# Attention in a four-part decoder trunk: one value product a pair of heads over 512 queries at causal widths, instead of two over 256

## The chip, the cores and the metric

The kernel runs on one core of one Trainium2 chip. The metric is the device time of one execution in microseconds, as a median of several runs. Below, PE is TensorE, DVE is VectorE, ACT is ScalarE, POOL is GpSimd and SP is SyncE, the engine that issues the loads of weights. All times and traces are of this chip.

## What is computed

The input is a sequence of 512 tokens with 1024 features, in float32. Two layers follow each other: an attention mixer with a gated feed-forward part, and a short-convolution mixer with the same feed-forward part. Only the attention mixer is changed:

```python
xn = rms_norm(h, norm_g)
proj = xn @ w_in                       # q, k, v of 16 heads of 64, and 8 gate logits
q_fox, k_fox, q_sb, k_sb = ...         # each head's q and k normalised over 64
# heads 0-7, forgetting attention:
logits = q @ k.T * scale + cum_f[q] - cum_f[k]        # causal: key <= query
out = softmax(logits) @ v
# heads 8-15, stick-breaking attention:
z = q @ k.T * scale                                   # strict: key < query
w = exp(log_sigmoid(z) + sum of log_sigmoid(-z) over later keys)
out = w @ v
h = h + concat(out) @ w_out
```

## The kernel before, in words

**Precision.** Every product of two float32 matrices is made of three matmuls. Each operand is split into a high part (`hi`, rounded to the type that PE reads fast, written by ACT) and the rest (`lo`, a subtraction on DVE); the matmuls are hi x hi, lo x hi and hi x lo (`mm3`, L246 to L252, and `mm3_rhs`, L502 to L505). Weights arrive by a DMA of 512 KB into `raw` and are split into `whi` and `wlo` (L227, L228).

**Layout.** Activations lie with features in partitions and the 512 tokens in columns. The 16 heads are worked on in 8 pairs, p = 0 to 7; pairs 0 to 3 are forgetting attention (`fox`), pairs 4 to 7 stick-breaking. Queries go in blocks of 128, b = 0 to 3.

**The steps of a pair.**
- `queries_keys(p)` makes K and Q of a pair: 24 matmuls of 512 columns for each (L248 to L250), an eviction with squares (L585, L593), then some microseconds of other work later the sums of squares (`sums`, L539), their turn (L547), the inverse roots on small tiles (`scales`, L549 to L568), and, ROWS microseconds later by the kernel's own counter, the turn of the widened scales (`rows`, L575) and the scaled Q and K (L577, L339, L340).
- `values(g)` makes V of four heads (two pairs): 4 blocks of 24 matmuls of 256 columns (L503 to L505).
- `logits(p, b)` makes the logits of one query block for both heads of a pair. Each head uses 64 of the array's 128 rows, so the two heads' matmuls run side by side (L610, L614). It goes on with the softmax (L625 to L630) or the stick-breaking weights (two sigmoids, a scan and a product, L634 to L640). Each head has its own tile `w`, and in stick-breaking its own `rest`.
- `turn(p, b)` turns a block's weights, 128 x 128 at a time, into a PSUM bank (L659) and splits them into the tiles `pt` (L662, L663). A `pt` tile holds two query blocks (256 queries) for 4 key blocks. The key blocks that the first of the two queries' blocks may not see are filled with zeros by POOL (L653).
- `weigh(p, half)` is the value product of 256 queries: for each head 2 (first half) or 4 (second half) key blocks, twice each for `hi` and `lo`, 256 columns wide (L678, L679). Both heads share one PSUM bank. The stationary operand is V's hi and lo side by side, so the two halves of the result are added (L688, L689) and split into `o_hi` and `o_lo`.
- `output` is the output projection of heads 0 to 7 with its residual add (L727), `output_part` that of heads 8 to 15.

**PSUM.** There are eight banks in three rings (`bank`, L69): "a" with two banks, "b" with four, "c" with two. K, Q, V, the value product and the output projection take "a"; logits take "b"; turns, sums and scales take "c".

**The order.** It is made by the kernel's own counter of PE time (`spend`, `after`, `fill`, L177 to L198). A loop over the 32 blocks issues the logits of block g, then FILL1 microseconds of other work (`fillers`: K, Q and V of later pairs, later the output projection), the value product of a block pair that is ready, the turns of block g - 1, then FILL2 microseconds of fillers. A scheduler below the kernel may move an instruction by some places. Weights are loaded in the order of a list (`want`).

Of the kernel before, what the change touches and what calls it, by code (L numbers as in the profile page):

```python
# [50 lines left out]
def trunk(  # L51
# [207 lines left out]
    class Norm:  # L259
# [222 lines left out]
    def values(g):  # L482
# [3 lines left out]
        for b in range(NB):  # L486
            acc = bank("a")
# [19 lines left out]
    rx2 = const.tile([P, NB], F32, tag="rx2", name="rx2")  # L507

    def square_norm():
        dve.tensor_tensor(rx2, norm.col, norm.col, op=ALU.mult)  # L510
        dve.tensor_scalar(rx2, rx2, 1.0 / HD, None, op0=ALU.mult)
# [8 lines left out]
    def queries_keys(p):  # L520
# [3 lines left out]
        v = tiny.tile([P, NB, 2, 2], F32, tag="qv", name=f"qv{p}")  # L524
        r = tiny.tile([P, NB, 2, 2], F32, tag="qr", name=f"qr{p}")
# [7 lines left out]
        def sums():  # L533
# [7 lines left out]
            flat = work.tile([P, 2 * P], F32, tag="flat", name=f"flat{p}", bufs=1)  # L541
# [13 lines left out]
        def scales():  # L555
            vf, rf = (t.rearrange("p b i h -> p (b i h)") for t in (v, r))
            dve.tensor_scalar(vf, vf, EPS, None, op0=ALU.add)
            rsqrt(rf, vf, 16, f"qk{p}")
            rf = r.rearrange("p b i h -> p b (i h)")
            dve.tensor_tensor(rf, rf, norm.col[:, :, None].to_broadcast([P, NB, 4]), op=ALU.mult)  # L560
            if not fox:
                s = q_scale[p] = aw.tile([P, 2, NB, 2], F32, tag="qscale", name=f"qscale{p}", bufs=3)
                dve.tensor_copy(s[:, 0], r[:, :, 1, :])
                dve.tensor_scalar(s[:, 1], r[:, :, 1, :], -1.0, None, op0=ALU.mult)
            wides = {}
            for i in kept:
                wides[i] = work.tile([P, S], F32, tag="u0", name=f"qwide{p}{i}").rearrange("p (b h d) -> p b h d", b=NB, h=2)
                dve.tensor_copy(wides[i], r[:, :, i, :][:, :, :, None].to_broadcast([P, NB, 2, HD]))  # L568
# [12 lines left out]
        for i in range(2):  # L581
            acc = bank("a")
# [12 lines left out]
        after(SUMS, sums)  # L595

    def logits(p, b):
# [20 lines left out]
        ws = []  # L618
        for e in range(2):
            s = ss[e]  # L620
            w = aw.tile([P, S], F32, tag="w", name=f"w{p}{b}{e}", bufs=WB)
            ws.append(w)
            if fox:
                top = tiny.tile([P, 1], F32, tag="top", name=f"top{p}{b}{e}")
                dve.reduce_max(top, s[:, 0:n], axis=AX.X, negate=True)  # L625
# [4 lines left out]
                dve.tensor_scalar(w[:, 0:n], w[:, 0:n], inv, None, op0=ALU.mult)  # L630
            else:
                scale = q_scale[p]
                rest = aw.tile([P, S], F32, tag="rest", name=f"rest{p}{b}{e}")
                act.activation(rest[:, 0:n], s[:, 0:n], AF.Sigmoid, scale=scale[:, 1, b, e:e + 1])  # L634
                act.activation(w[:, 0:n - 1], s[:, 0:n - 1], AF.Sigmoid, scale=scale[:, 0, b, e:e + 1])

                pool.memset(w[:, n - 1:n], 0.0)
                back = rest[:, 1:n][:, ::-1]
                dve.tensor_tensor_scan(back, back, begin[:, S - n + 1:S][:, ::-1], 0.0, op0=ALU.mult, op1=ALU.max)  # L639
                dve.tensor_tensor(w[:, 0:n - 1], w[:, 0:n - 1], rest[:, 1:n], op=ALU.mult)  # L640
        return ws
# [3 lines left out]
    def turn(p, b, ws):  # L645

        half, n = b // 2, (b + 1) * P
        if b % 2 == 0:
            pts[p, half] = []
            for e in range(2):  # L650
# [3 lines left out]
                pts[p, half].append(both)  # L654
        at_ = slice((b % 2) * P, (b % 2 + 1) * P)
        for e in range(2):
            t = bank("c")
            for k in range(b + 1):
                pe.transpose(t[:, k * P:(k + 1) * P], ws[e][:, k * P:(k + 1) * P], ident)  # L659
            src = t[:, 0:n].rearrange("p (k q) -> p k q", q=P)  # L660
            hi, lo = pts[p, half][e]
            act.activation(hi[:, 0:b + 1, at_], src, AF.Copy)  # L662
            dve.tensor_tensor(lo[:, 0:b + 1, at_], src, f32(hi[:, 0:b + 1, at_]), op=ALU.subtract)  # L663
        spend(0.22 * (b + 1))

    def weigh(p, half):
# [4 lines left out]
        acc = bank("a")  # L671
        to = slice(half * 256, (half + 1) * 256)
        last = 2 * half + 1
        for e in range(2):
            hi, lo = pts[p, half][e]
            for k in range(last + 1):
                w = v[:, k, 2 * (p % 2) + e].rearrange("p i d -> p (i d)")
                pe.matmul(acc[:, e * 256:(e + 1) * 256], w, hi[:, k, :], start=k == 0, stop=False)  # L678
                pe.matmul(acc[:, e * 256:(e + 1) * 256], w, lo[:, k, :], start=False, stop=k == last)  # L679
        spend(0.44 * (last + 1))  # L680
        if p == 4 and half == 0:
            o_tiles[1] = mixed(1)
        o_hi, o_lo = o_tiles[p // 4]
        total = work.tile([P, S], F32, tag="y", name=f"o{p}{half}")[:, 0:256]
        for e in range(2):
            own, other = (slice(i * HD, (i + 1) * HD) for i in (e, 1 - e))
            cols = slice(e * 256, (e + 1) * 256)
            act.activation(total[own, :], acc[other, cols], AF.Copy)  # L688
            dve.tensor_tensor(total[own, :], acc[own, cols], total[own, :], op=ALU.add)  # L689
        split(o_hi[:, p % 4, to], o_lo[:, p % 4, to], total)  # L690
# [120 lines left out]
    after(NORM0, lambda: (norm.scale(sums0), square_norm()))  # L811
# [6 lines left out]
    aw = attn.enter_context(tc.tile_pool(name="aw", bufs=2))  # L818

# [5 lines left out]
    dr = ap_.tile([P, S], F32R, tag="dr", name="dr")  # L825
# [6 lines left out]
    for g, ps_ in enumerate(((1, 2), (3, 4), (5, 6), (7,))):  # L832
# [6 lines left out]
    for g in range(len(blocks) + 2):  # L839
# [6 lines left out]
        if g >= 2 and blocks[g - 2][1] % 2:  # L846
            p, b = blocks[g - 2]
# [165 lines left out]
```

## Time and profile before

| | |
|---|---|
| runs of before | 1220.8, 1221.25, 1221.3 us, median 1221.25 |
| the profiled execution | 1220.77 us |
| its span, first to last instruction | 1219.0 us |
| TensorE's granted clock | 1.00 |
| attention | about 25 to 280 us of the span |

The profile shows one execution. A group's row has the line, the engine, the operation, tiles (out<-in), the shape, the count, then the busy time and the mean of one, and behind a bar the idle time of the engine just ahead of them with what ended it. A row of the timeline begins with the start and the duration. PE's rows overlap: a matmul starts while the one ahead is still in the pipeline, so the distance between starts is what a matmul costs in a stream, and the row's own length is not.

### The profile page before, as it was taken

The numbers are of one execution on the slowest core, as the hardware profiler recorded it, in microseconds if no ns is written. First come the engines' busy times: TensorE is split into PE (matmuls) and PEld (weight loads), VectorE is DVE, ScalarE is ACT, GpSimd is POOL, SyncE is SP. The second block draws the span as 40 slices with busy tenths as digits, with TensorE's granted clock in tenths as the row PEclk, the third lists the DMA queues.
The fourth block names the chain that finished last, engine by engine and source line by source line (L and its number), as shares of the span: only waits on it lengthen the run. The fifth ranks groups of instructions, "written<-read, shape, count | busy, mean of one in ns | idle before, by whom it ended". The sixth has DMA issues, their size and how long they took to land.

```text
span 1219.0 us, 15006 instructions
## 1 busy us (share of the span) xinstructions
PE 1204.0 (99%) x5841; PEld 973.4 (80%) x5841; DVE 762.8 (63%) x1250; ACT 503.4 (41%) x787; POOL 26.6 (2%) x139
## 2 busy tenths in 40 slices
PE   8999999999999999999999999999999999999998
PEld 7887877778888888888888888888888888888886
DVE  5887888887867777663333555465776767672222
ACT  6556576655544443432222222233434344442120
POOL 4000000000000000000000000000000000000000
PEclk9999999999999999999999999999999999999999
DMA  7312121213233333323333333323233332322330
GB/s 196 88 36 70 36 69 36 70 62 96 87 102 89 97 93 94 96 81 93 94 95 104 89 102 87 104 87 104 87 93 98 89 102 87 103 87 88 121 102 35
DMA packets 182696, 108.14 MB, mean 89 GB/s; under 512 B 4732, under 2 KB 175020, under 8 KB 182624
## 3 DMA queue, kind: packets, MB, share of 16 engines
q1 hardware_dynamic: 182080, 106.94, 29.7%
q8 instruction: 46, 0.75, 0.3%
q0 software_dynamic: 384, 0.17, 0.1%
q14 instruction: 26, 0.21, 0.1%
q10 hardware_dynamic: 160, 0.07, 0.0%
HBM read 105.06 MB, written 2.10 MB: 88 GB/s over the span
## 4 chain that ended last, share of the span: by engine, by line
PE 91%; DVE 6%; ACT 2%; issue 1%; DMA 0%; SPq 0%; DVEq 0%; POOL 0%; ACTq 0%
PE psa L248 13%; PE psa L250 12%; PE psa L249 12%; PE psb L248 12%; PE psb L250 12%; PE psb L249 12%; PE psa L503 2%; PE psa L504 2%; PE psa L505 2%; PE psb L504 2%; PE psb L503 2%; PE psb L505 2%; DVE rest L639 1%; PE psc L659 1%; PE psb L610 1%
## 5 line engine op out<-in xcount | busy, mean ns | idle before, releaser
L227 ACT ACTIVATE whi<-raw 128x1024 fp32r<-128x1024 f32 (+3 forms) x199 | 208.9, 1050 | 362.7 <-PE psb L249 134.9
L228 DVE TENSOR_TENSOR wlo<-raw,whi 128x1024 fp32r<-128x1024 f32 (+3 forms) x199 | 240.4, 1209 | 160.2 <-ACT whi L227 159.1
L248 PE MATMUL psa<-hs_hi,whi 128*128 128x512 f32 x544 | 219.4, 403 | 2.5 <-DVE o L689 1.3
L250 PE MATMUL psa<-hs_hi,wlo 128*128 128x512 f32 x544 | 215.1, 395 | 0.2 <-DVE wlo L228 0.2
L249 PE MATMUL psa<-hs_lo,whi 128*128 128x512 f32 x544 | 214.6, 395 | 0.0
L248 PE MATMUL psb<-hs_hi,whi 128*128 128x512 f32 x480 | 189.9, 396 | 0.0
L250 PE MATMUL psb<-hs_hi,wlo 128*128 128x512 f32 x480 | 189.8, 395 | 0.0
L249 PE MATMUL psb<-hs_lo,whi 128*128 128x512 f32 x480 | 188.7, 393 | 0.0
L347 DVE SCALAR_TENSOR_TENSOR u<-y,taps,u 128x510 f32<-128x510 f32 (+1 forms) x176 | 131.1, 748 | 3.3 <-ACT u L344 0.4
L248 PEld LDWEIGHTS psa<-hs_hi,whi 128*128 128x128 f32 x544 | 102.3, 188 | 25.7 <-issue 2.3
L250 PEld LDWEIGHTS psa<-hs_hi,wlo 128*128 128x128 f32 x544 | 102.2, 188 | 25.0 <-DVE wlo L228 1.1
L249 PEld LDWEIGHTS psa<-hs_lo,whi 128*128 128x128 f32 x544 | 102.3, 188 | 22.2 <-DVE hs_lo L758 0.4
L249 PEld LDWEIGHTS psb<-hs_lo,whi 128*128 128x128 f32 x480 | 90.1, 188 | 21.4
L250 PEld LDWEIGHTS psb<-hs_hi,wlo 128*128 128x128 f32 x480 | 90.1, 188 | 21.4
L248 PEld LDWEIGHTS psb<-hs_hi,whi 128*128 128x128 f32 x480 | 90.3, 188 | 20.2
L885 DVE TENSOR_TENSOR y<-psb,nrow_n 128x512 f32<-128x512 f32 x44 | 30.4, 691 | 83.3 <-PE psb L250 83.3
L339 ACT ACTIVATE a<-u 128x512 fp32r<-128x512 f32 x44 | 27.9, 634 | 118.7 <-DVE u L890 118.7
L889 ACT ACTIVATE u<-u 128x512 f32<-128x512 f32 x44 | 27.9, 633 | 91.3 <-DVE u L347 91.3
L344 ACT ACTIVATE u<-y,taps 128x512 f32<-128x512 f32 x88 | 63.1, 719 | 1.2 <-DVE y L885 1.1
L340 DVE TENSOR_TENSOR a<-u,a 128x512 fp32r<-128x512 f32 x44 | 30.5, 692 | 29.4 <-ACT a L339 29.4
L503 PE MATMUL psa<-whi,hs_hi 128*128 128x256 f32 (+1 forms) x128 | 38.3, 299 | 0.8 <-ACT qk L593 0.7
L505 PE MATMUL psa<-whi,hs_lo 128*128 128x256 f32 (+1 forms) x128 | 36.3, 283 | 0.0
(251 smaller groups left out, 1818.3 us busy)
## 6 DMA issues: line engine op xcount, KB each, us to landing
raw<-in_ffn_w_up SPq DMA_DIRECT2D x88, 512.0 KB, 3.8
raw<-in_ffn_w_down SPq DMA_DIRECT2D x30, 512.0 KB, 3.7
raw<-in_attn_w_in SPq DMA_DIRECT2D x24, 512.0 KB, 4.0
raw<-in_conv_w_in SPq DMA_DIRECT2D x24, 512.0 KB, 3.8
raw<-in_ffn_w_down SPq DMA_DIRECT2D x16, 448.0 KB, 3.6
raw<-in_attn_w_out SPq DMA_DIRECT2D x8, 512.0 KB, 3.5
raw<-in_conv_w_out SPq DMA_DIRECT2D x8, 512.0 KB, 3.9
x_tok<-in_x SPq DMA_DIRECT2D x4, 512.0 KB, 6.5
```

The costliest lines, as they stand in the source:

```text
L227: return (act.activation(hi[:, at_], raw[:, at_], AF.Copy), dve.tensor_tensor(lo[:, at_], raw[:, at_], f32(hi[:, at_]), op=ALU.subtract))
L228: dve.tensor_tensor(lo[:, at_], raw[:, at_], f32(hi[:, at_]), op=ALU.subtract))
L248: made = [pe.matmul(acc, w[0], rhs[0], start=first, stop=False), pe.matmul(acc, w[0], rhs[1], start=False, stop=False), pe.matmul(acc, w[1 ...
L249: pe.matmul(acc, w[0], rhs[1], start=False, stop=False),
L250: pe.matmul(acc, w[1], rhs[0], start=False, stop=last)]
L340: dve.tensor_tensor(lo, src, f32(hi), op=ALU.subtract)
L344: act.activation(dst, src, AF.Copy, scale=tap(2))
L347: dve.scalar_tensor_tensor(dst[:, d:], src[:, 0:S - d], tap(j), dst[:, d:], op0=ALU.mult, op1=ALU.add)
L503: pe.matmul(acc, lhs[0], w[0], start=first, stop=False)
L504: pe.matmul(acc, lhs[0], w[1], start=False, stop=False)
L505: pe.matmul(acc, lhs[1], w[0], start=False, stop=last)
L885: dve.tensor_tensor(y, acc, norm.row, op=ALU.mult)
```

## The change

- `weigh(p)` runs once a pair, over all 512 queries. Each head has a bank of its own. Key block k is multiplied with the queries of blocks k to 3 alone, so the widths are 512, 384, 256 and 128 columns.
- The turned weights of a pair lie packed in one tile per part, 20 blocks of 128 x 128 (10 for each head), with no zero blocks, and so without POOL's memsets. Head 0 has block (b, k) at 5b + k, so the queries' blocks of one key block are 5 places apart; head 1 has them at 19 - 6b + k, 6 places apart and backwards, which is why its result is read back in reversed block order. There is one such tile for each part; before there were two.
- `logits` puts both heads' weights into one tile, one for even and one for odd blocks. For blocks 0 and 1 the reciprocal (fox) and the last product (stick-breaking) are one operation for both heads. `rest` is one tile for the whole stage, with a column of zeros at its end that stands in for a memset a head.
- The scales are worked out from the sums of squares with `least` (mean square times EPS) added in the same operation; two small operations a pair go.
- K and Q from pair 1 on and V from group 1 on take ring "b". The value product keeps "a".
- ROWS is 8 instead of 5, FILL1 1.4 instead of 1.0, FILL2 2.2 instead of 2.6. K and Q of pair 5 come ahead of V for pairs 4 and 5, those of pair 7 ahead of V for pairs 6 and 7, in the fillers and in the list of loads.

```diff
-SUMS, FLAT, ROWS = 3.0, 1.5, 5.0
+SUMS, FLAT, ROWS = 3.0, 1.5, 8.0
-FILL1, FILL2, BEFORE = 1.0, 2.6, 2.0
+FILL1, FILL2, BEFORE = 1.4, 2.2, 2.0
...
-    for g, ps_ in enumerate(((1, 2), (3, 4), (5, 6), (7,))):
+    for g, ps_ in enumerate(((1, 2), (3, 4, 5), (6, 7), ())):
...
-            acc = bank("a")
+            acc = bank("b" if g >= 1 else "a")
...
-            dve.tensor_tensor(
-                v, t[:, 2 * P:4 * P].rearrange("p (i b c) -> p b i c", i=2, b=NB)[:, :, :, 0:2],
-                rx2[:, :, None, None].to_broadcast([P, NB, 2, 2]), op=ALU.mult,
+            dve.scalar_tensor_tensor(
+                v.rearrange("p i b h -> p (i b) h"), t[:, 2 * P:4 * P].rearrange("p (j c) -> p j c", c=32)[:, :, 0:2],
+                1.0 / HD, least[:, :, None].to_broadcast([P, 2 * NB, 2]), op0=ALU.mult, op1=ALU.add,
             )
...
-            dve.tensor_scalar(vf, vf, EPS, None, op0=ALU.add)
             rsqrt(rf, vf, 16, f"qk{p}")
-            rf = r.rearrange("p b i h -> p b (i h)")
-            dve.tensor_tensor(rf, rf, norm.col[:, :, None].to_broadcast([P, NB, 4]), op=ALU.mult)
...
-            acc = bank("a")
+            acc = bank("b" if p >= 1 else "a")
             yield from products(acc, weights())
...
+    def at_once(b):
+        return (slice(0, 2),) if b < 2 else (slice(0, 1), slice(1, 2))
...
-            w = aw.tile([P, S], F32, tag="w", name=f"w{p}{b}{e}", bufs=WB)
+        w = aw.tile([P, 2, (3 + b % 2) * P], F32, tag=f"w{b % 2}", name=f"w{p}{b}", bufs=1)[:, :, 0:n]
...
-                rest = aw.tile([P, S], F32, tag="rest", name=f"rest{p}{b}{e}")
+                rests.append(aw.tile([P, 2, S + 1], F32, tag="rest", name="rest", bufs=1))
...
-                pool.memset(w[:, n - 1:n], 0.0)
...
-                both = [aw.tile([P, NB, 256], F32R, tag=f"pt{i}", name=f"pt{p}{half}{e}{i}", bufs=PT) for i in range(2)]
-                for t in both:
-                    pool.memset(f32(t[:, 2 * half + 1, 0:P]), 0.0)
+            pts[p] = [aw.tile([P, 20, P], F32R, tag=f"pt{i}", name=f"pt{p}{i}", bufs=1) for i in range(2)]
...
+            to = (5 * b, 19 - 6 * b)[e]
+            hi, lo = (t_[:, to:to + b + 1, :].rearrange("p k q -> p (k q)") for t_ in pts[p])
+            act.activation(hi, t[:, 0:n], AF.Copy)
+            dve.tensor_tensor(lo, t[:, 0:n], f32(hi), op=ALU.subtract)
...
-    def weigh(p, half):
+    def weigh(p):
...
-                pe.matmul(acc[:, e * 256:(e + 1) * 256], w, hi[:, k, :], start=k == 0, stop=False)
-                pe.matmul(acc[:, e * 256:(e + 1) * 256], w, lo[:, k, :], start=False, stop=k == last)
+            acc = bank("a")
+            for k in range(NB):
+                w = v[:, k, 2 * (p % 2) + e].rearrange("p i d -> p (i d)")
+                first, step = ((6 * k, 5), (1 + k, 6))[e]
+                out_ = acc[:, k * P:] if e == 0 else acc[:, 0:(NB - k) * P]
+                for i, t in enumerate(pts[p]):
+                    pe.matmul(out_, w, t[:, first:first + step * (NB - k - 1) + 1:step, :], start=k == 0 and i == 0, stop=k == NB - 1 and i == 1)
...
-        if g >= 2 and blocks[g - 2][1] % 2:
+        if g >= 2 and blocks[g - 2][1] == NB - 1:
```

In the changed kernel the value product is at L682, the logits at L612 and L616, the turns at L658 and the turn of the widened scales at L573.

More of the change, by code (lines that the diff above doesn't have):

```diff
@@ L505, in mm3_rhs, with least_square @@
         pe.matmul(acc, lhs[1], w[0], start=False, stop=last)
[L507 to L511, printed above, removed]
+    least = const.tile([P, 2 * NB], F32, tag="least", name="least")
+    def least_square():
+        for i in range(2):
+            dve.tensor_scalar(least[:, i * NB:(i + 1) * NB], norm.mean, EPS, None, op0=ALU.mult)
     halves, q_scale, done = {}, {}, set()
@@ new lines, in logits @@
+        if fox:
+            top, total, inv = (tiny.tile([P, 2], F32, tag=t, name=f"{t}{p}{b}") for t in ("top", "total", "inv"))
+            for e in range(2):
+                dve.reduce_max(top[:, e:e + 1], ss[e][:, 0:n], axis=AX.X, negate=True)
+                act.activation(w[:, e, :], ss[e][:, 0:n], AF.Exp, bias=top[:, e:e + 1], accum_out=total[:, e:e + 1])
+            for es in at_once(b):
+                dve.reciprocal(inv[:, es], total[:, es])
+                for e in range(es.start, es.stop):
+                    dve.tensor_scalar(w[:, e, :], w[:, e, :], inv[:, e:e + 1], None, op0=ALU.mult)
+        else:
+            scale = q_scale[p]
+            if not rests:
+                rests.append(aw.tile([P, 2, S + 1], F32, tag="rest", name="rest", bufs=1))
+                pool.memset(rests[0][:, :, S:S + 1], 0.0)
+            rest = rests[0]
+            keys = slice(S - n, S)
+            for es in at_once(b):
+                for e in range(es.start, es.stop):
+                    act.activation(rest[:, e, keys], ss[e][:, 0:n], AF.Sigmoid, scale=scale[:, 1, b, e:e + 1])
+                    act.activation(w[:, e, :], ss[e][:, 0:n], AF.Sigmoid, scale=scale[:, 0, b, e:e + 1])
+                    back = rest[:, e, keys][:, ::-1]
+                    dve.tensor_tensor_scan(back, back, begin[:, keys][:, ::-1], 0.0, op0=ALU.mult, op1=ALU.max)
+                dve.tensor_tensor(w[:, es], w[:, es], rest[:, es, S - n + 1:S + 1], op=ALU.mult)
@@ L656, in turn @@
+        return w
+    pts = {}
+    def turn(p, b, w):
+        n = (b + 1) * P
+        if b == 0:
+            pts[p] = [aw.tile([P, 20, P], F32R, tag=f"pt{i}", name=f"pt{p}{i}", bufs=1) for i in range(2)]
         for e in range(2):
@@ L658, in turn @@
             for k in range(b + 1):
[L659 to L663, printed above, removed]
+                pe.transpose(t[:, k * P:(k + 1) * P], w[:, e, k * P:(k + 1) * P], ident)
+            to = (5 * b, 19 - 6 * b)[e]
@@ L664, in turn @@
+            hi, lo = (t_[:, to:to + b + 1, :].rearrange("p k q -> p (k q)") for t_ in pts[p])
+            act.activation(hi, t[:, 0:n], AF.Copy)
+            dve.tensor_tensor(lo, t[:, 0:n], f32(hi), op=ALU.subtract)
         spend(0.22 * (b + 1))
-    def weigh(p, half):
+    def weigh(p):
         need(("v", p // 2))
         v = v_tiles[p // 2]
[L671 to L681, printed above, removed]
+        if p == 4:
@@ L682, in weigh @@
             o_tiles[1] = mixed(1)
         o_hi, o_lo = o_tiles[p // 4]
-        total = work.tile([P, S], F32, tag="y", name=f"o{p}{half}")[:, 0:256]
+        total = work.tile([P, S], F32, tag="y", name=f"o{p}")
         for e in range(2):
-            own, other = (slice(i * HD, (i + 1) * HD) for i in (e, 1 - e))
-            cols = slice(e * 256, (e + 1) * 256)
-            act.activation(total[own, :], acc[other, cols], AF.Copy)
-            dve.tensor_tensor(total[own, :], acc[own, cols], total[own, :], op=ALU.add)
@@ L692, in output @@
+            src = acc.rearrange("p (b q) -> p b q", q=P)
+            if e:
+                src = src[:, ::-1, :]
+            own, other = (slice(i * HD, (i + 1) * HD) for i in (e, 1 - e))
+            to = total[own, :].rearrange("p (b q) -> p b q", q=P)
+            act.activation(to, src[other], AF.Copy)
+            dve.tensor_tensor(to, src[own], to, op=ALU.add)
+            spend(1.2)
+        split(o_hi[:, p % 4, :], o_lo[:, p % 4, :], total)
     def output(g, done):
@@ L818, in trunk @@
     aw = attn.enter_context(tc.tile_pool(name="aw", bufs=2))
+    rests = []
     o_tiles = {0: mixed(0)}
     dl = ap_.tile([P, 4, S], F32R, tag="dl", name="dl")
-    dr = ap_.tile([P, S], F32R, tag="dr", name="dr")
+    dr = aw.tile([P, 2, S + 1], F32, tag="rest", name="dr", bufs=1)[:, 0, 0:S].bitcast(F32R)
     sel = choose()
```

54 lines of the change are left out of this document (13 added, 41 removed).

## Prediction

> **What bounds the kernel now.** I read the page's engine shares first, then PE's waits, then the attention stage (25 to 280 us) by windows, then the timeline at each longer wait. From the page:
>
> ```profile
> span 1219.0 us, 15006 instructions
> PE 1204.0 (99%) x5841; PEld 973.4 (80%) x5841; DVE 762.8 (63%) x1250; ACT 503.4 (41%) x787; POOL 26.6 (2%) x139
> ```
>
> PE is the bound over the whole span. So there are only two kinds of gain: PE instructions that take less time, and gaps on PE that close. The next view is the busy time by engine in the attention stage, and one behind it for the feed-forward stages:
>
> ```profile
> 25.00:280.00 255.00, 247.10 (x1650) 199.98 (x1649) 206.53 (x519) 152.57 (x338) 14.34 (x93) 1.00 0.21 61
> 300.00:1200.00 900.00, 900.00 (x3909) 728.06 (x3908) 519.38 (x668) 317.91 (x398) 0.00 (x0) 1.00 0.32 94
> ```
>
> Columns are PE, PE's weight loads, DVE, ACT, POOL, granted clock, DMA share. From 300 us on PE has no gap, and the change touches nothing there. In attention PE idles 255 - 247.1 = 7.9 us, DVE is busy 81%, and the DMA engines 21%. The waits of PE between 25 and 280 us:
>
> ```profile
> PE psc L659 <- DVE pt L663: 1.7, 2, 1.4
> PE psa L248 <- DVE o L689: 1.6, 2, 1.3
> PE psc L575 <- DVE pt L663: 1.4, 2, 0.9
> PE psa L248 <- DVE h L727: 1.3, 1, 1.3
> PE psc L539 <- ACT sq L585: 0.5, 1, 0.5
> PE psc L575 <- DVE qwide L568: 0.5, 1, 0.5
> PE psc L539 <- DVE pt L663: 0.3, 1, 0.3
> PE psa L503 <- ACT qk L593: 0.3, 1, 0.3
> PE psa L678 <- DVE v L497: 0.2, 1, 0.2
> ```
>
> They add up to 7.8 us, the idle time of the window. All are waits for DVE or ACT to empty a PSUM bank or to hand over a tile; none is for a DMA.
>
> **The value product (term A).** The group of its matmuls, and how far apart such matmuls start (starts are the first column):
>
> ```profile
> L678 PE MATMUL psa<-pt,v 128*128 128x256 f32 x96 | 24.2, 288 | 0.2 <-DVE v L497 0.2
> L679 PE MATMUL psa<-pt,v 128*128 128x256 f32 x96 | 23.6, 282 | 0.0
> ```
> ```profile
> 83.88 0.28 PE L679 MATMUL psa<-pt,v 128*128 128x256 f32 x1
> 84.00 0.28 PE L678 MATMUL psa<-pt,v 128*128 128x256 f32 x1
> ...
> 87.87 0.34 PE L610 MATMUL psb<-qk_lo,qk_hi 64*128 64x384 f32 x2
> 88.04 0.35 PE L610 MATMUL psb<-qk_hi,qk_lo 64*128 64x384 f32 x2
> ...
> 89.74 0.60 PE L659 MATMUL psc<-ident,w 128*128 128x128 f32 x4
> ...
> 159.33 0.39 PE L250 MATMUL psa<-hs_hi,wlo 128*128 128x512 f32 x1
> 159.56 0.39 PE L248 MATMUL psa<-hs_hi,whi 128*128 128x512 f32 x1
> ```
>
> A row's duration (0.28 us) is no price, since the next matmul starts while it runs. The distance of starts is: 0.12 us for 256 columns, 0.17 for 384 (two half-height matmuls side by side), 0.23 for 512. Four turns (128 columns) take 0.60 and one alone 0.28, so they are (0.60 - 0.28)/3 = 0.11 apart. Before, 192 x 0.12 = 23.0 us. After, a head has widths 512, 384, 256, 128, twice each: 32 of each width over 16 heads, 32 x (0.23 + 0.17 + 0.12 + 0.11) = 20.2 us. **A = -2.8 us.** No normal matmul of 128 columns in these types stands in the trace. Its bounds are half of the 256-column distance, 0.06 (A = -4.4), and the 512-column one, 0.23, if a narrow one were no cheaper (A = +1.0). I take the turns' 0.11: same width, same array, one weight load each.
>
> The Trainium skill's "TensorE: Matmul & The Clock Gate" (Back-to-back issue gap) gives an isolated gap of N/2.4 + 2.5 ns, 56 ns for N = 128, as an estimate 32 x 0.05 = 1.7 us less than A. Its section on LDWEIGHTS gives P/1.2 ns, 107 ns for 128 columns; the turns' 0.11 agrees with this one, and so A goes by it.
>
> **The waits (term B).** The two longest are these:
>
> ```profile
> 211.54 0.55 DVE L663 TENSOR_TENSOR pt<-psc,pt 128x384 fp32r<-128x384 f32 x1
> 212.12 0.43 DVE L689 TENSOR_TENSOR o<-psa,o 64x256 f32<-64x256 f32 x1
> ...
> 212.69 0.47 PE L248 MATMUL psa<-hs_hi,whi 128*128 128x512 f32 x1 [1.32 <-DVE o L689]
> ```
> ```profile
> 235.54 1.22 DVE L639 TENSOR_TENSOR_SCAN rest<-rest,begin 128x511 f32<-128x511 f32 x1
> ...
> 236.67 0.66 DVE L727 TENSOR_TENSOR h<-psa,h 128x512 f32<-128x512 f32 x1
> ...
> 237.39 0.50 PE L248 MATMUL psa<-o_hi,whi 128*128 128x512 f32 x1 [1.28 <-DVE h L727]
> ```
>
> In the first, the accumulator of Q and K wants a bank of ring "a" that the value product still holds, and its eviction stands in DVE's queue behind a turn's. In the second, the output projection wants one whose residual add stands behind a scan. After the change Q, K (from pair 1) and V (from group 1) take ring "b" with four banks, and each pair is evicted once. Wait by wait:
> - L689 to Q/K: its 1.3 of the 1.6 go. The output projection stays in "a" and keeps 0.3.
> - L727: I leave 1.3. The second head's product is a new user of "a" (below) and can wait for just such an add.
> - L575, all three (1.9): ROWS goes from 5 to 8, which puts some 3 us of products between the scales and the turns. They go.
> - L659 (1.7): DVE's row of the half pair's eviction no longer stands there at every second block; I take the longer one off, 1.4.
> - L497 and L593 (0.5): accumulators that now have four banks. They go.
> - L539 (0.8): stays.
>
> So 1.3 + 1.9 + 1.4 + 0.5 = 5.1 us go, in seven waits. Each cost PE more than its idle time, since a 0.28 us row runs 0.16 us past the next start: 7 x 0.16 = 1.1. Against that I put new waits. DVE's queue loses 76 rows of 1,238 and ACT 20 of 747, but a pair's eviction is now one burst at double width, and joined operations hand over later; I take one wait as long as the longest above, 1.4 + 0.16 = 1.6. **B = -5.1 - 1.1 + 1.6 = -4.6 us**, bounds -7.8 - 1.4 = -9.2 (all go, with nine restarts) and 0 (they only move).
>
> On the new user of "a", PE in pair 6 with the output projection of group 0 running (psa_3050 its accumulator, psa_3058 and psa_3069 the two heads' products), before and after:
>
> ```order
> L250 MATMUL psa198_3416<-o_hi0_357,wlo26_3195 128x512
> L678 MATMUL psa201_3448<-pt6100_3261,v3_2667 128x256
> L679 MATMUL psa201_3448<-pt6101_3262,v3_2667 128x256
> L678 MATMUL psa201_3448<-pt6100_3261,v3_2667 128x256
> L679 MATMUL psa201_3448<-pt6101_3262,v3_2667 128x256
> ```
> ```order
> L682 MATMUL psa_3058<-pt_2811,v_2634 128x128
> L682 MATMUL psa_3058<-pt_2812,v_2634 128x128
> L658 MATMUL psc_3084<-ident,w_2985 128x128
> L658 MATMUL psc_3088<-ident,w_2985 128x128
> L248 MATMUL psa_3050<-o_hi_357,whi_2916 128x512
> L249 MATMUL psa_3050<-o_lo_358,whi_2916 128x512
> L250 MATMUL psa_3050<-o_hi_357,wlo_2917 128x512
> L248 MATMUL psa_3050<-o_hi_357,whi_2916 128x512
> L249 MATMUL psa_3050<-o_lo_358,whi_2916 128x512
> L250 MATMUL psa_3050<-o_hi_357,wlo_2917 128x512
> L682 MATMUL psa_3069<-pt_2811,v_2634 128x512
> L682 MATMUL psa_3069<-pt_2812,v_2634 128x512
> ```
>
> Before, all 16 matmuls of a half pair stand together in one bank (the first four are shown). After, the second head comes behind the accumulator's last matmul and takes a bank as soon as DVE has emptied one: everything behind it on PE waits too. This place is where L727's 1.3 us may come back.
>
> **Fewer interruptions (term C).** Logits matmuls use half of the array's rows, two side by side. A lone one shows what a visit costs:
>
> ```profile
> 161.42 0.40 PE L250 MATMUL psa<-hs_hi,wlo 128*128 128x512 f32 x1
> 161.74 0.38 PE L610 MATMUL psb<-qk_hi,qk_lo 64*128 64x256 f32 x1
> 162.05 0.50 PE L248 MATMUL psa<-hs_hi,whi 128*128 128x512 f32 x1
> 162.39 0.39 PE L249 MATMUL psa<-hs_lo,whi 128*128 128x512 f32 x1
> ```
>
> From 161.42 to 162.39 pass 0.97 us; two 512-column matmuls alone take 0.46. Beside the lone matmul's own 0.12 that is 0.39 a visit. On PE, around the first blocks of pair 4, order before and after (qk tiles of logits; psc turned weights of pair 3; psa_2228 and psb_2038 products):
>
> ```order
> L610 MATMUL psb_2301<-qk_lo_2115,qk_hi_1882 128x256
> L610 MATMUL psb_2302<-qk_lo_2115,qk_hi_1882 128x256
> L659 MATMUL psc_2275<-ident,w_2151 128x128 x4
> L610 MATMUL psb_2301<-qk_hi_2114,qk_lo_1883 128x256
> L659 MATMUL psc_2282<-ident,w_2159 128x128 x3
> L248 MATMUL psa_2228<-hs_hi,whi_1887 128x512
> ```
> ```order
> L505 MATMUL psb120_2038<-whi17_1870,hs_lo_112 128x256
> L612 MATMUL psb124_2116<-qk_hi40_1931,qk_hi41_1713 128x256
> L612 MATMUL psb125_2117<-qk_hi40_1931,qk_hi41_1713 128x256
> L612 MATMUL psb124_2116<-qk_lo40_1932,qk_hi41_1713 128x256
> L612 MATMUL psb125_2117<-qk_lo40_1932,qk_hi41_1713 128x256
> L612 MATMUL psb124_2116<-qk_hi40_1931,qk_lo41_1714 128x256
> L612 MATMUL psb125_2117<-qk_hi40_1931,qk_lo41_1714 128x256
> L503 MATMUL psb120_2038<-whi17_1870,hs_hi_111 128x256
> ```
>
> Before, the block's last two matmuls are torn apart, and the partner of the one shown comes 27 rows later by itself: it is the lone one of 161.74. After, all six stand together. Counted over PE's whole order there are 38 visits before and 35 after, and four matmuls without a partner before and none after. **C = -3 x 0.39 - 4 x 0.12 = -1.7 us**, bounds -3 and 0.
>
> **At nothing.** POOL issues 96 rows fewer (135 to 39), the memsets; it waited, nobody on PE for it. The scales' arithmetic loses two small DVE operations a pair, inside term B. SP issues the same 212 loads, pair 5's weights now ahead of values of group 2; PE's list has no wait for a load, and the DMA engines have 79% to spare; if that cover went, one load late by a matmul block would cost a wait of the lengths above. The last pair's evictions (one chain, wider) lie under 33 output matmuls, 33 x 0.23 = 7.6 us; the widest rows that stand in such a chain are under 0.7 us and there are six.
>
> **Sum.** A + B + C = -2.8 - 4.6 - 1.7 = -9.1 us, on the profiled execution of 1220.77 us (its span 1219.0, 1.8 outside): 1211.7. The median of the runs shown lies 0.5 higher, 1221.25, so the forecast for a median is **1212.2**. A measurement of this kernel can tell 0.2% (2.4 us) from no change.
>
> **Rivals.**
> 1. *Narrow matmuls are no cheaper.* The 128-column product costs as much as the 512-column one: 32 x 0.12 = +3.8, **1216.0**. For: the kernel pads its own logits to 256 columns, and the trace has no narrow normal matmul. Against: turns at 0.11. Chance 0.2.
> 2. *All product matmuls slow down.* Their moving operand is now blocks of 128 columns picked at a stride of five or six blocks, and no row shows such an operand. At 0.23 for each of the 128, A becomes 29.4 - 23.0 = +6.4, 9.2 more: **1221.4**, no change. The Trainium skill's "Advanced Engine Details and Errata" (PSUM Cachelines) warns that a non-contiguous access slows matmuls significantly but asks only for two neighbours in a row; here 128 stand together, and no run here shows it. Chance 0.04.
> 3. *Waits only move.* B = 0: **1216.8**. For: DVE at 81% sets every handover, and it loses only 6% of its rows. Chance 0.16.
> 4. *Slower: single buffers.* Both heads' weights now share one tile per parity, one "rest" tile serves all blocks, and the turned weights have one buffer where there were two. If a block's chain on DVE ends after PE wants its turns, PE stops at L658. A stop costs 1.4 + 0.16; it takes (9.1 + 2.4)/1.56, about 8 of the 32 blocks, to end slower by more than can be told. With ten it is **1227.8**. Against: a block comes every 255/32 = 8 us, and FILL1 + FILL2 + FILL1 between logits and their turns grows from 4.6 to 5.0. Chance 0.06.
>
> **How the numbers follow.** Forecast 0.54, the rivals 0.2, 0.04, 0.16, 0.06. The likeliest case's own range is A -4.4, B -9.2 and C -3 at their ends together, which is not likely; half of the way from the sum to these ends (-16.6) gives -12.8, or 1208.5. Upwards it reaches past rivals 1 and 3, so **1208.5 to 1217.5**. Faster by over 0.2%: 0.54 + 0.2 + 0.16 = 0.9; same: 0.04; slower: 0.06.
>
> **What would show it.** Right: PE's 32 rows of 128 columns 0.11 apart; PE idle between 25 and 280 us near 7.9 - 5.1 + 1.4 = 4.2 us; no L248 wait for an "o" row; no lone L612; the first matmul of the feed-forward stage some 9 us earlier, and nothing gained behind it. Wrong: product rows over 0.2 us apart at 128 columns (rival 1), at every width (2), as much idle time under other names (3), or L658 waiting at many blocks (4).

## The result and the profile after

The changed kernel takes **1209.7 us** (median of four runs, 1209.23 to 1210.82); the kernel before took 1221.28 us in the runs beside it (1220.8 to 1221.31). The ratio is 0.9907, with a 95% interval of 0.9892 to 0.9922: 11.6 us or 0.9% faster. The forecast was 1212.2 us with a range of 1208.5 to 1217.5; the measurement lies inside it, 2.5 us below the forecast.

The head of the page of the changed kernel, and its windows over attention and over the feed-forward stages (PE, weight loads, DVE, ACT, POOL, granted clock, DMA share, GB/s):

```profile
span 1208.2 us, 14599 instructions
PE 1199.0 (99%) x5777; PEld 970.0 (80%) x5777; DVE 753.4 (62%) x1194; ACT 498.8 (41%) x763; POOL 12.0 (1%) x44
```
```profile
25.00:280.00 255.00, 252.49 (x1641) 205.43 (x1640) 208.22 (x480) 157.49 (x328) 0.63 (x2) 1.00 0.23 65
300.00:1189.00 889.00, 889.00 (x3855) 718.90 (x3854) 511.93 (x649) 313.80 (x394) 0.00 (x0) 1.00 0.32 94
```

The span is 10.8 us shorter. PE's idle time in attention falls from 7.9 us to 255 - 252.49 = 2.5 us. Behind 300 us PE still has no gap: all that was gained was gained in attention and is kept. What PE still waits for between 25 and 280 us:

```profile
PE psc L658 <- DVE qn L575: 1.0, 1, 1.0
PE psc L658 <- DVE pt L662: 0.9, 2, 0.5
PE psc L573 <- DVE pt L662: 0.4, 1, 0.4
PE psc L540 <- DVE pt L662: 0.2, 1, 0.2
```

No L248 row waits for an evicted bank, neither of the value product nor of the output projection. In attention PE stops where turns (L658), turned scales (L573) or sums (L540) want a bank of ring "c" that DVE has not read yet. So 5.4 of the 10.8 us between the two profiled executions are idle time. The others must be in matmuls that follow each other faster.

For the value product, a row of the timeline holds a whole pair; the price of the pair is the distance from its start to the start of the next row:

```profile
80.03 2.64 PE L682 MATMUL psa<-pt,v 128*128 128x512 f32 x16
82.51 0.41 PE L658 MATMUL psc<-ident,w 128*128 128x128 f32 x2
```

From the first of the 16 matmuls to what follows them pass 2.48 us. Before, a pair had 24 matmuls 0.12 apart, 2.88 us. That is 0.40 a pair, 3.2 us over eight pairs. Summed over all distances of matmul starts, less idle time, the product falls from 23.6 to 20.2 us, 3.4 us, which is the better figure: not every row stands at the typical distance. The logits, with the mask's matmuls, fall from 27.8 to 26.4.

A wait costs PE more than its idle time: that counts only from where the matmul ahead has run out, and in a stream the next one would have started before. Against the typical distance of such matmuls that is 0.15 to 0.33 us more at each wait over 0.05 us: 2.7 us for 14 waits before, 1.2 us for seven after. Of the 1.4 us of the logits, 0.9 are such restarts, at four waits right behind logits.

### The profile page after: what moved, and what is told of

Read it like the earlier page. It is cut to its first block, busy times and chain, and to the rows that moved or that the text cites. A ratio compares the mean times of both kernels' runs of the same rounds, so it can differ in the third digit from the quotient of the medians.

```text
span 1208.2 us, 14599 instructions
## 1 busy us (share of the span) xinstructions
PE 1199.0 (99%) x5777; PEld 970.0 (80%) x5777; DVE 753.4 (62%) x1194; ACT 498.8 (41%) x763; POOL 12.0 (1%) x44
## 4 chain that ended last, share of the span: by engine, by line
PE 96%; DVE 1%; ACT 1%; DMA 1%; issue 0%; SPq 0%; DVEq 0%; ACTq 0%
PE psb L248 14%; PE psb L250 14%; PE psb L249 14%; PE psa L248 11%; PE psa L250 11%; PE psa L249 11%; PE psb L503 3%; PE psb L504 2%; PE psb L505 2%; PE psa L503 2%; PE psa L504 2%; PE psa L505 2%; PE psb L612 2%; PE psc L658 1%; PE psa L682 1%; DMA x_tok<-in_x 1%
## 5 line engine op out<-in xcount | busy, mean ns | idle before, releaser
L248 PE MATMUL psb<-hs_hi,whi 128*128 128x512 f32 x592 | 237.6, 401 | 0.0
L250 PE MATMUL psb<-hs_hi,wlo 128*128 128x512 f32 x592 | 234.1, 395 | 0.0
L249 PE MATMUL psb<-hs_lo,whi 128*128 128x512 f32 x592 | 233.0, 394 | 0.0
L248 PE MATMUL psa<-hs_hi,whi 128*128 128x512 f32 x432 | 171.5, 397 | 0.4 <-ACT whi L227 0.4
L250 PE MATMUL psa<-hs_hi,wlo 128*128 128x512 f32 x432 | 170.8, 395 | 0.3 <-DVE wlo L228 0.2
L249 PE MATMUL psa<-hs_lo,whi 128*128 128x512 f32 x432 | 170.4, 395 | 0.0
L248 PEld LDWEIGHTS psb<-hs_hi,whi 128*128 128x128 f32 x592 | 111.5, 188 | 24.6 <-issue 1.2
L249 PEld LDWEIGHTS psb<-hs_lo,whi 128*128 128x128 f32 x592 | 111.3, 188 | 24.5
L250 PEld LDWEIGHTS psa<-hs_hi,wlo 128*128 128x128 f32 x432 | 81.2, 188 | 20.2 <-DVE wlo L228 1.1
L248 PEld LDWEIGHTS psa<-hs_hi,whi 128*128 128x128 f32 x432 | 81.2, 188 | 19.3 <-ACT whi L227 0.8
L891 ACT ACTIVATE u<-u 128x512 f32<-128x512 f32 x44 | 27.8, 632 | 91.2 <-DVE u L347 91.2
L340 DVE TENSOR_TENSOR a<-u,a 128x512 fp32r<-128x512 f32 x44 | 30.5, 692 | 29.4 <-ACT a L339 29.4
L503 PE MATMUL psa<-whi,a 128*128 128x512 f32 x88 | 35.5, 403 | 0.0
L503 PE MATMUL psb<-whi,a 128*128 128x512 f32 x88 | 34.9, 396 | 0.0
```

What stands on the lines that cost most here:

```text
L248: made = [pe.matmul(acc, w[0], rhs[0], start=first, stop=False), pe.matmul(acc, w[0], rhs[1], start=False, stop=False), pe.matmul(acc, w[1 ...
L249: pe.matmul(acc, w[0], rhs[1], start=False, stop=False),
L250: pe.matmul(acc, w[1], rhs[0], start=False, stop=last)]
L340: dve.tensor_tensor(lo, src, f32(hi), op=ALU.subtract)
L503: pe.matmul(acc, lhs[0], w[0], start=first, stop=False)
```

## The experiments

Three questions were open. What does a 128-column matmul cost? (In the trace the second of two starts 0.06 us after the first, the matmul after it 0.11 later, so either could be the price.) Which edits take the waits away? Do they do it alone, or only together? Each kernel was timed against the kernel before; "PE idle" is that of the window from 25 to 280 us of its profiled execution.

| kernel | what it is | median us | PE idle us |
|---|---|---|---|
| before | | 1221.28 | 7.9 |
| after | the change | 1209.70 | 2.5 |
| narrow_x4 | after, 96 narrow matmuls more | 1219.62 | 1.8 |
| narrow_logits | after, first block's logits not padded | 1212.72 | 6.7 |
| banks_a | after, ring "a" | 1213.64 | 3.9 |
| rows5 | after, ROWS 5 | 1211.96 | 4.2 |
| fills_old | after, old fills | 1210.47 | 3.3 |
| order_old | after, old order of pairs | 1212.76 | 4.7 |
| product_only | after, the four above undone together | 1218.75 | 7.2 |
| sched_only | before, with those four done | 1218.35 | 7.8 |
| halves | after, two products a pair | 1218.04 | 8.6 |
| small_undone | after, small operations apart | 1211.52 | 4.1 |
| sched_fill | sched_only with FILL1 1.6 | 1212.93 | 4.7 |
| fill_more | after, FILL1 1.6, ROWS 7.5 | 1207.63 | 1.1 |

The kernel before, timed beside each of them, had medians of 1221.22 to 1221.33 us. Single times of `product_only`, `sched_only`, `halves` and `sched_fill` lie up to 2.8 us apart, those of the others up to 1.6, so a difference under about 1 us between two medians is not read.

### The price of a narrow matmul

`narrow_x4` issues each product matmul of 128 columns four times:

```diff
                 for i, t in enumerate(pts[p]):
-                    pe.matmul(out_, w, t[...], start=k == 0 and i == 0, stop=k == NB - 1 and i == 1)
+                    for again in range(4 if k == NB - 1 else 1):
+                        pe.matmul(out_, w, t[...], start=k == 0 and i == 0, stop=k == NB - 1 and i == 1 and again == 3)
```

> The changed kernel with each product matmul of 128 columns issued four times instead of once (96 more; the last block of 128 queries of each head gets its last key block four times). Theory (128 columns cost 0.06 us): 96 x 0.06 = 5.8 us more, 1215.5 us. Rival 1 (0.11 us, the weight load's time as in the prediction): 10.6 us more, 1220.3 us. Rival 2 (no cheaper than 0.23 us): 22 us more, 1232 us.

Measured: 1219.62 us, 9.9 more than the changed kernel, 0.10 us for each of the 96 (0.11 with the 0.7 us that PE idles less). The same pair in its timeline:

```profile
79.18 3.99 PE L683 MATMUL psa<-pt,v 128*128 128x512 f32 x28
83.00 0.40 PE L658 MATMUL psc<-ident,w 128*128 128x128 f32 x2
```

3.82 us instead of 2.48 for twelve matmuls more: 0.112 us each. The theory of 0.06 falls, rival 1 holds: narrow matmuls in a row follow each other at 0.11 us, and so do the starts of their weight loads in the trace, each some 0.06 ahead of a matmul's. The 0.06 between two matmuls is real but comes once, at the second one behind wide matmuls. That the loads have run ahead there, so that it finds its weights ready, fits these rows; no run tests it by itself. The Trainium skill's "TensorE: Matmul & The Clock Gate" (LDWEIGHTS) gives P / 1.2 ns for a load of P columns, as an estimate 107 ns for 128, near the measured 112. The sustained 81 ns that the Trainium skill's "TensorE: Matmul & The Clock Gate" (Back-to-back issue gap) states for N = 128 isn't reached here in a row.

`narrow_logits` tries the same price on half-height matmuls:

```diff
-        wide = max(n, 256)
+        wide = n
```

> The changed kernel with the first block's logits 128 columns wide instead of padded to 256. The four-fold product matmuls showed 0.10 us for a 128-column matmul in a row, and the pairs of 256-column logits stand 0.114 us apart. Theory (the weight load sets the distance of narrow matmuls): nothing, 1209.7 us. Rival (half-height loads are short, the pairs stand 0.06 us apart): 20 distances inside the eight visits x 0.055 = 1.1 us less, 1208.6 us. A second rival, the padding is there because a narrow one costs more: 1211 us or more.

The first visit of logits, pairs side by side, in `narrow_logits` and in the changed kernel:

```profile
50.99 0.33 PE L612 MATMUL psb<-qk_hi,qk_hi 64*128 64x128 f32 x2
51.15 0.28 PE L612 MATMUL psb<-qk_lo,qk_hi 64*128 64x128 f32 x2
51.27 0.28 PE L612 MATMUL psb<-qk_hi,qk_lo 64*128 64x128 f32 x2
51.38 0.27 PE L616 MATMUL psb<-dr,dl 64*128 64x128 f32 x2
```
```profile
51.82 0.39 PE L612 MATMUL psb<-qk_hi,qk_hi 64*128 64x256 f32 x2
52.04 0.28 PE L612 MATMUL psb<-qk_lo,qk_hi 64*128 64x256 f32 x2
52.16 0.28 PE L612 MATMUL psb<-qk_hi,qk_lo 64*128 64x256 f32 x2
52.28 0.28 PE L616 MATMUL psb<-dr,dl 64*128 64x256 f32 x2
```

Half the columns, and from the second pair on they still stand 0.11 to 0.12 us apart: there the price of the theory holds. Only the first distance is shorter, 0.16 instead of 0.22. The theory's time does not come: 1212.72 us, 3.0 more than the changed kernel, and the second rival's number. But its reason isn't the second rival's, since no narrow row is dearer. The edit also went into the kernel's own counter (`spend(... * wide * ...)`), so the fillers behind it moved, and PE idles 6.7 us instead of 2.5. That the counter is the reason is argued and not shown, as no run held it fixed. It was not foreseen, and it is the first sign of how much the waits hang on the exact order.

### Ring, ROWS, fills and order, one at a time

```diff
# banks_a
-            acc = bank("b" if g >= 1 else "a")
+            acc = bank("a")
...
-            acc = bank("b" if p >= 1 else "a")
+            acc = bank("a")
# rows5
-SUMS, FLAT, ROWS = 3.0, 1.5, 8.0
+SUMS, FLAT, ROWS = 3.0, 1.5, 5.0
# fills_old
-FILL1, FILL2, BEFORE = 1.4, 2.2, 2.0
+FILL1, FILL2, BEFORE = 1.0, 2.6, 2.0
# order_old, here and in the list of loads
-((1, 2), (3, 4, 5), (6, 7), ())
+((1, 2), (3, 4), (5, 6), (7,))
```

> The changed kernel with K, Q and V back in ring a, nothing else. Theory (ring b lets an accumulator start while an earlier one is evicted, and logits are not torn apart by it): waits of K, Q and V for evicted banks return, 38 visits and some lone logits, 2 to 5 us more than the changed kernel, 1212 to 1215 us, PE idle 4 to 7 us. Rival (ROWS, fills and order take the waits away, the ring does nothing): 1209.5 to 1210.5 us, idle 2.5 us.

Measured: 1213.64 us, 3.9 more, in size as the theory had it. Its four longest waits:

```profile
PE psa L682 <- DVE v L497: 1.0, 2, 0.6
PE psc L658 <- DVE qn L575: 1.0, 1, 1.0
PE psc L573 <- DVE pt L662: 0.9, 1, 0.9
PE psa L682 <- DVE qk_lo L588: 0.6, 1, 0.6
```

Idle time explains 1.4 of the 3.9. Here it is the value product (L682) that waits for banks which K, Q and V hold. PE's order again has 38 visits of logits instead of 35, and the logits' distances sum to 27.8 us instead of 26.4: another 1.4, of which 0.4 are restarts. The rest of the 3.9 is not assigned.

> The changed kernel with ROWS 5 instead of 8. Ring, ROWS, fills and order together are worth 9.0 us there (1218.75 against 1209.7), the ring alone 3.9, so 5.1 are left for the other three. Theory (the turns of the widened scales wait on DVE, L573, as in the prediction): 1.9 us more, 1211.6 us, with two or three waits at L573. Rival 1 (one of fills and order carries the 5.1): 1209.7 us. Rival 2 (ROWS carries them): 1214 us or more.

Measured: 1211.96 us, 2.3 more. The waits at the turned scales are back where the prediction had them:

```profile
PE psc L573 <- DVE pt L662: 2.6, 3, 1.2
```

> The changed kernel with FILL1 1.0 and FILL2 2.6 instead of 1.4 and 2.2. Theory (the chain from logits to turns gets FILL1 + FILL2 + FILL1, 4.6 instead of 5.0 us of other work, so turns wait more at L658): 1 to 2 us more, about 1211.2 us. Rival 1 (nothing by it): 1209.7 us. Rival 2 (it carries the 5.1 us): 1214 us or more.

Measured: 1210.47 us (1210.24 to 1211.63). The 0.8 more can't be told from nothing.

> The changed kernel with the old order of pairs, K and Q of pair 5 behind V of group 2 and of pair 7 behind V of group 3, in fillers and loads. Theory (a pair's K and Q that come late put their scaling into DVE's queue between a block's weights, and PE waits there): 1 to 2 us more, about 1211.2 us. Rival 1 (nothing by it): 1209.7 us. Rival 2 (it carries the 5.1 us): 1214 us or more.

Measured: 1212.76 us, 3.1 more and 2.2 us more idle time. The theory was right in sign and low in size, and its mechanism is not shown: the wait behind a scaled Q (L658 <- qn L575) is 1.0 us, as in the changed kernel. What is new is a wait of 1.0 us at L248 behind the residual add, the prediction's L727, and more at turns (1.5 us in three). One by one the four are worth 3.9 + 2.3 + 0.8 + 3.1 = 10.1 us in the changed kernel.

### Each side of the change alone

> The changed kernel with K, Q and V back in ring a, ROWS 5, FILL1 and FILL2 1.0 and 2.6 and the old order of pairs; the packed weights, the product over 512 queries and the joined operations stay. Theory (the product saves by its widths, 128 columns at 0.06 us; the waits belong to ring and order): only the product's 3.4 us go, 1218 us, PE idle between 25 and 270 us 6 to 8 us, 38 visits of logits on PE as before. Rival 1 (the waits go because a pair is evicted once and small blocks' operations are joined): idle near 2.5 us, 1211 to 1213 us. Rival 2 (the second head's product waits in ring a behind the accumulators): idle over 9 us, 1220 us or more.

Measured: 1218.75 us, 2.5 less than before; PE idles 7.2 us. The four schedule edits together are therefore worth 9.0 us beside the new product, about the sum of the four single ones. The theory holds for the waits. Alone, the new product brings no more than its own rows, 2.5 us where these give 3.4. The idle time did not go; its longest waits are others:

```profile
PE psc L658 <- DVE pt L662: 1.9, 1, 1.9
PE psc L658 <- DVE qv L550: 1.5, 1, 1.5
PE psc L573 <- DVE pt L662: 1.2, 3, 0.5
PE psa L503 <- DVE o L689: 0.9, 2, 0.6
PE psa L682 <- DVE o L689: 0.7, 2, 0.4
```

> The kernel before with K, Q (from pair 1) and V (from group 1) in ring b, ROWS 8, FILL1 and FILL2 1.4 and 2.2 and the new order of pairs; product, memsets and operations as before. Theory: the waits go and the visits of logits fall from 38 to 35 without the product, 5 to 7 us less, 1214.5 to 1216 us, PE idle 2 to 4 us. Rival 1 (the waits need the single eviction and the joined operations): idle stays at 6 to 8 us, 1220 to 1221 us.

Measured: 1218.35 us, 2.9 less than before; idle 7.8 us. The theory falls. No accumulator waits for a bank any more, but five turns of a block's weights do in its place, 5.0 us in all. So the two sides bring 2.5 and 2.9 us alone, and 11.6 together: 6.2 us are in neither alone.

### Why only together

Three pieces of the product side could hold the missing 6 us: the single product and eviction of a pair, the joined small operations, or neither, if the schedule's constants just did not suit the old operations. `halves` puts two products of 256 queries back, at causal widths and from the packed weights, each with its own eviction:

```diff
-    def weigh(p):
+    def weigh(p, half):
...
+        acc = bank("a")
+        b0, b1 = 2 * half, 2 * half + 1
+        for e in range(2):
+            for k in range(b1 + 1):
+                low = max(k, b0)
+                n = b1 - low + 1
+                first, step = ((5 * low + k, 5), (19 - 6 * b1 + k, 6))[e]
```

> The changed kernel with two value products a pair again, each for 256 queries with both heads in one bank of ring a and an eviction of its own; packed weights, causal widths, joined operations, rings, ROWS, fills and order stay. By widths a pair has 16 matmuls of 256 columns and 8 of 128, 128 x 0.12 + 64 x 0.09 = 21.1 us, 0.9 more than the changed kernel. Theory (the waits that schedule and product take away only together hang on one product and one eviction a pair): 0.9 plus 3 to 6 us of waits, 1214 to 1216.5 us, PE idle 5 to 8 us between 25 and 270 us. Rival (they hang on the joined operations and fewer DVE rows): 1210.6 us, idle near 2.5 us.

Measured: 1218.04 us, 8.3 more; idle 8.6 us. Here are four of the waits of `sched_only`, then four of `halves`, from their timelines:

```profile
169.54 0.44 PE L659 MATMUL psc<-ident,w 128*128 128x128 f32 x2 [0.96 <-DVE qn L577]
195.96 0.44 PE L659 MATMUL psc<-ident,w 128*128 128x128 f32 x2 [0.92 <-DVE pt L663]
225.17 0.66 PE L575 MATMUL psc<-ident,qwide 128*128 128x128 f32 x4 [1.03 <-DVE pt L663]
259.20 0.66 PE L659 MATMUL psc<-ident,w 128*128 128x128 f32 x4 [1.40 <-DVE pt L663]
```
```profile
167.79 0.44 PE L658 MATMUL psc<-ident,w 128*128 128x128 f32 x2 [0.97 <-DVE qn L575]
194.07 0.44 PE L658 MATMUL psc<-ident,w 128*128 128x128 f32 x2 [0.90 <-DVE pt L662]
223.74 0.66 PE L573 MATMUL psc<-ident,qwide 128*128 128x128 f32 x4 [0.83 <-DVE pt L662]
257.80 1.12 PE L658 MATMUL psc<-ident,w 128*128 128x128 f32 x8 [1.70 <-DVE pt L662]
```

They are the same waits, at the same operations 1.4 to 1.9 us earlier, of much the same length, though `halves` has all the joined operations and packed tiles. The longest of each is not among them: at 235.31 `sched_only` waits 1.56 us at a turn (L659), at 234.06 `halves` 1.94 us at L248 for its own eviction (L691). What the two kernels share, and the changed one has not, is a product and an eviction in the middle of each pair. Does DVE's row of that eviction make the wait at 195.96? This is what stands ahead of it in `sched_only`, then ahead of the same turns (192.57) in the changed kernel:

```profile
191.76 0.56 ACT L634 ACTIVATE rest<-psb,qscale 128x384 f32<-128x384 f32 x1
192.10 0.42 DVE L340 TENSOR_TENSOR o_lo<-o,o_hi 128x256 fp32r<-128x256 f32 x1
192.44 0.95 DVE L639 TENSOR_TENSOR_SCAN rest<-rest,begin 128x383 f32<-128x383 f32 x1
...
195.49 0.42 DVE L663 TENSOR_TENSOR pt<-psc,pt 128x256 fp32r<-128x256 f32 x1
```
```profile
188.38 0.58 ACT L640 ACTIVATE rest<-psb,qscale 128x384 f32<-128x384 f32 x1 [0.71 <-PE psb L612]
189.00 0.96 DVE L643 TENSOR_TENSOR_SCAN rest<-rest,begin 128x384 f32<-128x384 f32 x1 [0.60 <-ACT rest L640]
...
192.09 0.42 DVE L662 TENSOR_TENSOR pt<-psc,pt 128x256 fp32r<-128x256 f32 x1
...
192.57 0.44 PE L658 MATMUL psc<-ident,w 128*128 128x128 f32 x2 [0.54 <-DVE pt L662]
```

In both, a block's two scans and products stand ahead of the eviction of a turn's bank. In `sched_only` the first scan starts behind the half pair's last row (L340), but that row hardly holds it: the scan starts 0.11 us behind the end of ACT's sigmoid (L634), and 0.03 behind it in the changed kernel, where nothing of an eviction stands there. From the first scan to the turn pass 3.52 and 3.57 us, as good as the same. What differs is PE's own work between the block's logits and this turn: ten matmuls of 512 columns in the changed kernel, nine in `sched_only` and in `halves`. PE comes to the turn 0.29 us later by it, most of the 0.38 us between waits of 0.92 and 0.54.

The wait at 169.54 tells the same. Ahead of it, in `sched_only` and in `halves`, PE has 17 matmuls of 256 columns, four turned scales and two turns behind the logits; where the changed kernel has the same, at another block, it waits as long:

```profile
221.29 0.44 PE L658 MATMUL psc<-ident,w 128*128 128x128 f32 x2 [1.00 <-DVE qn L575]
```

So at these two places it is the order on PE that makes the wait, and not a second eviction in DVE's queue. That a second product in each pair changes this order is what `halves` shows; how the kernel's counter comes to it was not followed.

`small_undone` takes the small operations apart and leaves the single product:

```diff
-        return (slice(0, 2),) if b < 2 else (slice(0, 1), slice(1, 2))
+        return (slice(0, 1), slice(1, 2))
...
+            dve.tensor_scalar(vf, vf, 0.0, None, op0=ALU.add)
             rsqrt(rf, vf, 16, f"qk{p}")
+            dve.tensor_scalar(rf, rf, 1.0, None, op0=ALU.mult)
...
-            act.activation(to, src[other], AF.Copy)
-            dve.tensor_tensor(to, src[own], to, op=ALU.add)
+            for c in (slice(0, 2), slice(2, 4)):
+                act.activation(to[:, c], src[other, c], AF.Copy)
+                dve.tensor_tensor(to[:, c], src[own, c], to[:, c], op=ALU.add)
```

> The changed kernel with the small operations taken apart again: reciprocal and product of blocks 0 and 1 for each head, two small DVE operations more in each pair's scales, and each eviction of the product in two parts of 256 columns; 56 DVE rows more. Theory (they are not what the waits hang on): 1209.5 to 1210.5 us. Rival (DVE's fewer rows take the waits away): idle back to 5 us or more, 1213 us or more.

Measured: 1211.52 us, 1.8 more; idle 4.1 us. That is between theory and rival: 56 rows more make DVE busy 760.6 us instead of 753.4, ACT has 24 more, and PE idles 1.6 us longer. The joined operations are not free of effect, as the theory had them, but they do not hold the 6 us. Which of the three parts it is was not tried.

`sched_fill` asks whether the old operations only want other constants. To `sched_only` it adds one:

```diff
-FILL1, FILL2, BEFORE = 1.4, 2.2, 2.0
+FILL1, FILL2, BEFORE = 1.6, 2.2, 2.0
```

> The kernel before with ring b, ROWS 8 and the new order, as sched_only (1218.35 us), but FILL1 1.6 and FILL2 2.2. Theory 1 (only one product a pair makes the schedule pay): 1218 us again, idle near 7.8 us. Theory 2 (the fill constants of sched_only did not suit its order; 0.2 us more of other work between logits and turns of a block takes waits at L659 away): 1214 to 1215.5 us, idle 4 to 5 us.

Measured: 1212.93 us, 5.4 less than `sched_only`, with the old product and all its evictions; idle 4.7 us (in an execution of 1214.11). Theory 2 holds, and by more than it expected. What is left of the long waits:

```profile
PE psc L659 <- DVE pt L663: 1.8, 1, 1.8
PE psc L575 <- DVE pt L663: 1.3, 1, 1.3
PE psc L539 <- DVE pt L663: 1.0, 2, 0.7
```

So the single product is one way to be rid of these waits, and not the only one: with two products a pair they are there at FILL1 1.4, and at 1.6 most of them are gone. Why 1.6 suits that order, and whether `halves` would gain by it too, was not tried. With FILL1 1.6 the schedule side alone is worth 8.3 us (1221.2 to 1212.9), and the changed kernel lies another 3.2 below (1209.7). That this is near what the product's rows gave is chance: 2.2 of the 3.2 us are idle time (4.7 against 2.5), and the changed kernel gains by FILL1 1.6 too, as the next run shows.

### A version that beats both

In nearly every fence above PE waits at turns, and 0.2 us more of other work between logits and turns took such waits away in `sched_fill`. `fill_more` gives the changed kernel FILL1 1.6 and ROWS 7.5.

> The changed kernel with FILL1 1.6 (1.4) and ROWS 7.5 (8.0). Its waits that are left are turns that wait for a block's weights at L658 and L573; FILL1 1.0 with FILL2 2.6 cost 0.8 us. Theory (more other work between logits and turns): 1 to 2 us less, 1207.7 to 1208.7 us. Rival (0.4 us of fills a block run out of fillers earlier and other waits come): 1210 us or more.

Measured: **1207.63 us** (1207.23 to 1208.32), ratio to before 0.989, interval 0.9876 to 0.9903; its slowest run is 0.9 us under the fastest of the changed kernel. PE idles 1.1 us in attention, and of the turns none waits:

```profile
25.00:280.00 255.00, 253.88 (x1648) 207.22 (x1647) 210.08 (x481) 158.76 (x330) 0.63 (x2) 1.00 0.23 66
```
```profile
PE psc L540 <- DVE pt L662: 0.7, 1, 0.7
PE psa L248 <- DVE h L728: 0.2, 1, 0.2
```

Which of the two constants does it was not separated. `sched_fill`, which also has FILL1 1.6 but ROWS 8, is 5.3 us slower, and that is about the product side's worth where both have the longer fill.

## Why the prediction was right, and where it was off

- **Term A (-2.8)** came out at -3.4 by the sum of all distances. The product after takes 20.2 us, as added up; the one before took 23.6 and not 23.0, since seven of its rows, next to matmuls of another kind, stand 0.19 to 0.22 apart. The disputed piece, 0.11 us for 128 columns taken from the turns, was right as the price in a row (0.10 to 0.11, `narrow_x4`). In the product it is 0.10, (2.48 - 2 x 2 x (0.23 + 0.17 + 0.12)) / 4.
- **Rivals 1 and 2** fall by the same rows: a narrow matmul does not cost 0.23, and the blocks picked at a stride of five or six cost by their width (0.23, 0.17, 0.12), as contiguous ones do.
- **Term B (-4.6)** is the one most mis-sized: idle time fell by 5.4 us and the restarts by 1.5, together -6.9. By place, PE's waits before and after are: accumulators and product (L248, L503, L678) 3.4 and 0; turned scales 1.9 and 0.4; sums 0.8 and 0.2; turns of weights 1.7 and 1.9. So the steps that failed are the waits left in: the residual add's 1.3 (L727), the output projection's 0.3 and 0.6 of the sums went too. The first hangs on the exact order, since `order_old` has 1.0 us of it and `narrow_logits` 0.6.
- **The burst and ROWS, inside term B.** For the turns, 1.4 was taken off and 1.4 put back as a new wait from the eviction's double-width burst; the total was near, the reason was not. The longest wait, 1.00 at L658, has no eviction ahead of it: it waits for the scaled Q (L575) behind two scans, and DVE stood idle for 0.61 us just before these. ROWS 8 does not remove the scales' waits by itself either: `sched_only` has it and three of them, 2.0 us, while `rows5` brought three back in the changed kernel.
- **What term B did not see** is that it added up waits as if each belonged to one edit. The runs show otherwise: done alone, either side leaves 7 to 8 us of idle time under other names. That is **rival 3**, "waits only move", and it is what happens to each half of the change. It was wrong for the whole, whose constants suit its order better; the prediction gave them no price of their own, while 0.2 us of FILL1 moved `sched_only` by 5.4 us.
- **Term C (-1.7)** was over-sized. The logits' distances fell by 1.4 us, with 35 visits for 38, but 0.9 of that are restarts behind four waits and belong to term B; 0.5 is left for the visits. The count hangs on ring "b": `banks_a` has 38.
- **Rival 4** did not come: three of the 32 blocks wait at L658, for 1.9 us in all.
- **Rows.** The prediction counts 76 rows fewer on DVE and 20 on ACT; the profiles show 56 (1250 to 1194) and 24 (787 to 763). Nothing in its sum uses them.
- **Sum.** 3.4 + 5.4 + 1.5 + 0.5 = 10.8 us, the difference of the two profiled spans; smaller pieces, up to 1.1 us each, cancel. The forecast's 9.1 lies near partly by luck: A and B were 0.6 and 2.3 us too small, C 1.2 too large. The rest of the 2.5 us is the step from the profiled execution to the median: 0.5 up was forecast, 0.2 down was measured.

## What to carry to other kernels

Where one engine is busy 97% and waits for a second one that is busy 81%, as PE and DVE were in attention before, a wait is a meeting of two queues: an edit that removes its cause may only move the meeting, so try the schedule's constants again after each such edit, for the old version too, before crediting the edit. Price narrow matmuls by a measured row of them: from 256 columns down to 128 almost nothing is saved here (0.117 to 0.112 us). And when an experiment changes a size, see whether the size also feeds the planner that orders the work; if it does, hold the planner's number fixed, or the run measures the order.

## What the runs showed of the hardware

- A 128-column matmul in these types costs 0.112 us in a row, hardly less than one of 256 columns (0.117), at full height (`narrow_x4`) and at half height (`narrow_logits`). Only the second behind wider ones starts after 0.06.
- A moving operand of 128-column blocks at a stride of 5 or 6 blocks costs no more than a contiguous one: 0.23, 0.17 and 0.12 us for 512, 384 and 256 columns.
- A wait on PE costs 0.15 to 0.33 us beyond its idle time: 2.7 us in all for the 14 waits before, 1.2 for the seven after.
- 56 small rows more on DVE, 7.2 us of busy time, went with 1.8 us more in this kernel (`small_undone`).
